# Running maxima of the scores in PSUM, later accumulating transfers, and a new chunk order in a fused attention block

## The chip, the core and the metric

The kernel runs on one core of a Trainium2 chip. The time is the device time of one execution in microseconds; the lower the better. A core has a matrix engine (TensorE, PE in the profile, with PEld for its weight loads), VectorE (DVE), ScalarE (ACT), GpSimd (POOL) and SyncE (SP), which issues transfers. Each runs its own queue in order; they wait for each other with semaphores. SBUF is the memory that they all work in, PSUM the small memory into which TensorE writes its products and which DVE and ACT can read and write too.

## The reference

One decoder block, batch 1, 1024 tokens with 16 learned meta tokens ahead of them (1040 rows), width 1024, all in float32.

```python
h = rmsnorm(concat([meta, x]), norm_g)
u_pool, z_pool, q, k, v, z_attn, f_logit, g_pool, g_attn = split(h @ w_in)
y_pool = causal_multiscale_pool(u_pool, pool_w, pool_scale) * silu(z_pool)
log_f  = log_sigmoid(f_logit + b_forget)
# logit[t, s] = q_t . k_s / 8 + sum of log_f over s < j <= t, causal; 8 heads of 64
y_attn = forgetting_attention(q, k, v, log_f) * silu(z_attn)
merged = sigmoid(g_pool) * (y_pool @ w_up_pool) + sigmoid(g_attn) * (y_attn @ w_up_attn)
out = rmsnorm(concat([meta, x]) + merged @ w_out, final_norm_g)[16:]
```

## The kernel before

**Arithmetic.** A float32 matrix is split into two parts of a reduced format, a rounded one and the rest (hh and hl of the normed rows, whi and wlo of a weight), and a product is three matmuls: hh x whi, hl x whi, hh x wlo. ACT makes whi (L156), POOL makes wlo with four subtractions of 256 columns (L158).

**Attention.** There are 16 units: four pairs of heads, two heads each, and two halves of 512 queries. A unit of the first half (even number) has five blocks of 128 keys, one of the second half (odd number) nine. `qk` makes the scores of one block: two matmuls (L680, L681) into one of two PSUM buffers ps, an addition of bias and mask on DVE for the diagonal part (L687), and an evacuation with bias on ACT (L689) into S in SBUF. The running maximum m over the blocks is an SBUF tile: at the second block DVE takes the maximum of the first two S (L693 copies columns that the second block doesn't reach, L694), and later m and S (L696). `maxes` finds the maximum over keys: DVE transposes m in squares of 32 (L701), reduces (L703), ACT swaps halves and quarters (L705, L708) with maxima on DVE between them (L706, L709), and DVE writes the result, spread over partitions, into a PSUM tile of the pool psT (L711). That pool has two buffers, called pt. `soft` subtracts it from S (L720), takes the exponential on ACT (L721), splits the result in ph (ACT, L724) and pl (DVE, L725, which reads S and ph, both in SBUF), adds up the denominators on POOL (acc, L730 to L733), and `av` multiplies ph and pl with V (L741) into po. `finish` copies po to SBUF (L748), stores both halves of it apart (y and y2, L750; their sum is wanted), and sums acc (L752, L754).

**Order.** PE's queue is written by hand: while unit i does `soft`, unit i+1 does `qk`, block by block, and a filler F puts matmuls of the input projection between the steps, also behind each unit's maxima, with the evacuations and splits that they need. The order on DVE, ACT, POOL and SP comes from a scheduler, bounded by `after` (stay behind an instruction in the same queue) and `behind` (wait for an instruction of another engine).

**Sums of blocks.** The gates' and the output's products are done as a 2 x 2 block scheme with seven products instead of eight, which needs sums of blocks of weights and of activations. They are made in device memory: SP stores blocks (put), ACT and POOL make negated blocks (neg, L602 and L604), and accumulating transfers on POOL's queue (`add`, L590, and `add_y`, L618, which sums y and y2 of a pair) add one to another. A table SUMS says which belong to which unit; `sums_of(i)` runs after `finish` of unit i, and the transfers stay behind the last acc addition in POOL's queue.

**Last block product.** Behind the attention come the block products (`g_prod`, L967) in four chunks of 512 rows each, whose PSUM tiles ga_[0..2] are pj buffers (three of them) and ga_[3] a pt buffer. The values that were in these buffers, the gate z of the pooling branch, are added to zp (`plus_`, L982, DVE) before the buffers are written again. `pool_mm(i)` multiplies the pooled values with their map and scales them (L848) into zp[i]; the last of the seven products, number 6, alternates with `pool_mm`, a chunk after a map. `up_weights` loads and splits a block of the next stage's weights (whu on ACT, L1098; wlu on DVE, L1099).

Of the kernel before, what the change touches and what calls it, by code (L numbers as in the profile page):

```python
# [8 lines left out]
F32 = mybir.dt.float32  # L9
F32R = mybir.dt.float32r  # L10
AF = mybir.ActivationFunctionType
ALU = mybir.AluOpType
# [42 lines left out]
def tile_hybrid_block(ctx, tc, x, meta, norm_g, w_in, b_forget, pool_w, pool_scale,  # L55
# [123 lines left out]
    def run(g):  # L179
        for _ in g:  # L180
            pass
# [406 lines left out]
    def add(dst, src):  # L588
        d, r = [t.rearrange("(p k) c -> p (k c)", k=4) for t in (dst, src)]
        after(nc.gpsimd.dma_start(d, r, accum_op=ALU.add, max_dma_last_dim=8192), accs[-1])  # L590
# [25 lines left out]
    def add_y(p):  # L616
        d, r = [spill[n, p].rearrange("(p k) c -> p (k c)", k=2) for n in ("y", "y2")]
        after(nc.gpsimd.dma_start(d, r, accum_op=ALU.add, max_dma_last_dim=8192), accs[-1])  # L618
# [26 lines left out]
    class Unit:  # L645
# [19 lines left out]
        def qk(self, b):  # L665
# [5 lines left out]
            if b == 0:  # L671
                self.m = ap_.tile([KB, 512], F32, name="m")
# [18 lines left out]
            if b == 1:  # L691
                if c0:
                    nc.vector.tensor_copy(m[:, :c0], S0[:, :c0])  # L693
                nc.vector.tensor_tensor(m[:, c0:], S0[:, c0:], s[:, c0:], op=ALU.max)  # L694
            elif b > 1:
                nc.vector.tensor_tensor(m[:kb, c0:], m[:kb, c0:], s[:kb, c0:], op=ALU.max)  # L696

        def maxes(self, extra=0.0):
            F.pull(LM1 + extra)
            mt = ap_.tile([KB, 512], F32, name="mt")  # L700
            nc.vector.transpose(mt, self.m)  # L701
            r, x, r2, y, mx = [sm.tile([128, 16], F32, name=n) for n in ("mr", "mx", "ms", "my", "mz")]
# [41 lines left out]
        def finish(self):  # L744
# [3 lines left out]
            nc.scalar.activation(t, po, AF.Copy)  # L748
            for n, part in (("y", hr), ("y2", lr)):
                nc.sync.dma_start(spill[n, self.p][hr, self.q0:self.q0 + 512], t[part])  # L750
# [35 lines left out]
    run(v_blocks(0, (6, 9), (0, 1)))  # L786
    units = [Unit(p, e, half) for p in range(4) for e in range(2) for half in range(2)]
    merged(list(units[0].a_steps()), [])
    units[0].maxes(FIRST)
    for i, u in enumerate(units):  # L790
# [11 lines left out]
        if nxt is not None:  # L802
            nxt.maxes()
        u.finish()
        sums_of(i)
        if i % 4 == 1 and i > 1:
            add_y(i // 4 - 1)
# [188 lines left out]
    add_y(3)  # L996
# [130 lines left out]
    ws[0, 0] = up_weights(0, 0)  # L1127
    plus_(zp[0][:, T1_], ga_[0])
    silu(zp[0][:, T1_], zp[0][:, T1_], -1.0)
    for i in range(4):  # L1130
        pool_mm(3 - i)
        g_prod(ga_[i], 6, i, False)
        if i:
            silu(za[i - 1][:, T1_], ga_[i - 1])
        if i < 2:
            rows_[i, 0] = gate_row(i, 0)
    silu(za[3][:, T1_], ga_[3])
# [209 lines left out]
```

## Time and profile before

| what | value |
|---|---|
| median of 3 runs | 745.23 us (744.98 to 746.96) |
| the profiled execution's own time | 744.3 us |
| its span in the profile | 742.6 us, mean granted clock of TensorE 0.996 |
| PE, PEld busy | 720.2 us (97%), 616.6 us (83%) |
| DVE, ACT, POOL busy | 536.5 us (72%), 417.0 us (56%), 334.4 us (45%) |

The page gives busy times of each engine; the idle time of an engine that isn't the bottleneck costs nothing. A row of a timeline reads: start in us, length in us, engine, line, operation, output <- inputs, shape, and x with the number of instructions that the row holds; in brackets the idle time of the engine before it, and the tile and engine that ended it. A row of groups has the count, then busy time in us, the mean of one in ns, and the idle time before them. Names in the profile leave out numbers: m, S, pt, pl and zp are the tiles above, pj a PSUM buffer of the projections.

### The profile page before, as it was taken

How to read it: one execution, taken by the hardware profiler on the slowest of the kernel's cores; microseconds unless marked ns; L12 is line 12 of the kernel's file. 1: busy time of each engine (PE TensorE's matmuls, PEld its weight loads, DVE VectorE, ACT ScalarE, POOL GpSimd, SP SyncE). 2: the span in 40 equal slices, each digit the busy share in tenths (PEclk: the TensorE clock that was granted, in tenths of full speed). 3: DMA queues.
4: the chain of work that ended last, by engine and by line, in shares of the span. 5: the costliest groups of instructions: out<-in, count | busy, mean ns of one | idle time of the engine just before them, and what ended most of it. 6: DMA issues, size and time to landing. Idle time of an engine off the chain costs nothing.

```text
span 742.6 us, 10841 instructions
## 1 busy us (share of the span) xinstructions
PE 720.2 (97%) x3637; PEld 616.6 (83%) x3637; DVE 536.5 (72%) x917; ACT 417.0 (56%) x914; POOL 334.4 (45%) x410
## 2 busy tenths in 40 slices
PE   8999999999999899999999999999989999999996
PEld 6997989997888797898988878888868888888885
DVE  4743577777889687887877858875876554887775
ACT  6752567565675666576765566342764432626445
POOL 4412245658336584365543766473843001005243
PEclk9999999999999999999999999999999999999999
DMA  9301125897864975738475586495905457672006
GB/s 285 77 26 32 29 67 194 206 330 170 221 194 92 237 202 161 192 68 208 124 173 120 134 214 229 117 342 174 307 16 170 143 184 258 222 266 76 0 1 227
DMA packets 88906, 120.45 MB, mean 162 GB/s; under 512 B 11377, under 2 KB 54385, under 8 KB 86786
## 3 DMA queue, kind: packets, MB, share of 16 engines
q1 hardware_dynamic: 85216, 100.36, 43.0%
q0 software_dynamic: 2336, 16.78, 12.2%
q10 hardware_dynamic: 1298, 2.63, 0.9%
q8 instruction: 28, 0.46, 0.3%
q14 instruction: 28, 0.23, 0.1%
HBM read 93.33 MB, written 54.72 MB: 199 GB/s over the span
## 4 chain that ended last, share of the span: by engine, by line
PE 71%; DVE 9%; ACT 8%; issue 4%; DMA 1%; POOL 0%; POOLq 0%; DVEq 0%; ACTq 0%; SPq 0%
PE pj L170 45%; PE pj L1227 8%; PE pj L967 6%; PE po L741 4%; PE pt L1227 2%; DVE pl L725 2%; PE pt L967 2%; PE ps L680 2%; ACT S L689 2%; PE ps L681 2%; ACT S L721 1%; ACT ph L724 1%; PE pj L515 1%; DVE m L696 1%; ACT whi L156 1%
## 5 line engine op out<-in xcount | busy, mean ns | idle before, releaser
L170 PE MATMUL pj<-hh,whi 128*128 128x512 f32 (+3 forms) x640 | 145.6, 354 | 0.0
L170 PE MATMUL pj<-hh,wlo 128*128 128x512 f32 (+3 forms) x640 | 143.6, 351 | 0.0
L170 PE MATMUL pj<-hl,whi 128*128 128x512 f32 (+3 forms) x640 | 142.7, 352 | 0.0
L158 POOL TENSOR_TENSOR wlo<-raw,whi 128x256 fp32r<-128x256 f32 x116 | 91.7, 871 | 97.9 <-ACT whi L156 41.5
L170 PEld LDWEIGHTS pj<-hl,whi 128*128 128x128 f32 x640 | 108.9, 190 | 12.0
L170 PEld LDWEIGHTS pj<-hh,whi 128*128 128x128 f32 x640 | 108.8, 190 | 11.8
L170 PEld LDWEIGHTS pj<-hh,wlo 128*128 128x128 f32 x640 | 108.6, 190 | 11.5
L725 DVE TENSOR_TENSOR pl<-S,ph 128x512 fp32r<-128x512 f32 (+4 forms) x112 | 89.3, 811 | 21.2 <-ACT ph L724 20.8
L733 POOL TENSOR_TENSOR acc<-acc,S 128x272 f32<-128x272 f32 (+4 forms) x80 | 76.7, 959 | 12.5 <-ACT S L721 6.6
L689 ACT ACTIVATE S<-ps,negc 128x400 f32<-128x400 f32 (+2 forms) x96 | 48.7, 515 | 47.9 <-DVE S L687 44.4
L696 DVE TENSOR_TENSOR m<-m,S 128x272 f32<-128x272 f32 (+4 forms) x80 | 47.6, 595 | 21.1 <-ACT S L689 18.9
L721 ACT ACTIVATE S<-S 128x512 f32<-128x512 f32 (+4 forms) x112 | 49.3, 478 | 17.2 <-DVE S L720 17.0
L724 ACT ACTIVATE ph<-S 128x512 fp32r<-128x512 f32 (+4 forms) x112 | 52.3, 479 | 7.2 <-PE po L741 6.9
L136 POOL TENSOR_TENSOR gw<-graw,gw 128x256 fp32r<-128x256 f32 x40 | 44.3, 1187 | 23.5 <-ACT gw L947 14.6
L720 DVE TENSOR_TENSOR S<-S,pt 128x512 f32<-128x512 f32 (+4 forms) x112 | 50.7, 498 | 0.6
L967 PE MATMUL pj<-gh,gw 128*128 128x512 f32 x180 | 43.7, 400 | 2.6 <-DVE zp L982 2.6
L680 PE MATMUL ps<-qa,ka 128*128 128x512 f32 (+4 forms) x112 | 37.6, 335 | 7.7 <-ACT S L689 7.5
L1120 DVE TENSOR_TENSOR rl<-pj,rl 128x512 f32<-128x512 f32 x32 | 22.0, 690 | 30.3 <-PE pj L170 30.2
L967 PEld LDWEIGHTS pj<-gh,gw 128*128 128x128 f32 x180 | 34.9, 194 | 10.5 <-issue 3.0
L156 ACT ACTIVATE whi<-raw 128x512 fp32r<-128x512 f32 x58 | 33.9, 622 | 12.6 <-PE pj L170 6.2
L741 PE MATMUL po<-pl,V 128*128 128x512 f32 (+4 forms) x112 | 38.1, 340 | 2.9 <-DVE pl L725 2.6
L731 POOL TENSOR_TENSOR acc<-S 128x400 f32<-128x400 f32 (+1 forms) x16 | 20.0, 1250 | 41.5 <-ACT S L721 41.4
(228 smaller groups left out, 1345.1 us busy)
## 6 DMA issues: line engine op xcount, KB each, us to landing
raw<-in_w_in_dram SPq DMA_DIRECT2D x31, 512.0 KB, 5.9
gs<-in_w_in_dram SPq DMA_DIRECT2D x5, 1024.0 KB, 6.9
td<-in_w_out_dram SPq DMA_DIRECT2D x5, 1024.0 KB, 10.6
xt<-in_x_dram SPq DMA_DIRECT2D x8, 512.0 KB, 7.8
sp_y<-t SPq DMA_DIRECT2D x32, 128.0 KB, 2.6
gs<-gs POOLq DMA_DIRECT2D x4, 1024.0 KB, 8.7
sp_gp<-st SPq DMA_DIRECT2D x16, 256.0 KB, 4.7
td<-td POOLq DMA_DIRECT2D x4, 1024.0 KB, 8.4
```

Of the source, the lines that this page charges most:

```text
L158: ins = nc.gpsimd.tensor_tensor(lo[:, k:k + 2], raw[:, k:k + 2], r32(hi[:, k:k + 2]), op=ALU.subtract)
L170: nc.tensor.matmul(ps, a, b, start=(i == 0), stop=(i == len(seq) - 1))
L680: nc.tensor.matmul(ps[:kb, c0:], ka[:, k0:k0 + kb], qa[:, q0 + c0:q0 + 512], start=True, stop=False)
L689: nc.scalar.activation(s[:kb, f0:], ps[:kb, f0:], AF.Identity, bias=nb_)
L696: nc.vector.tensor_tensor(m[:kb, c0:], m[:kb, c0:], s[:kb, c0:], op=ALU.max)
L721: exps.append(nc.scalar.activation(s[:kb, c0:], s[:kb, c0:], AF.Exp))
L724: nc.scalar.activation(ph[:kb, c0:], s[:kb, c0:], AF.Copy)
L725: dves.append(nc.vector.tensor_tensor(pl[:kb, c0:], s[:kb, c0:], r32(ph[:kb, c0:]), op=ALU.subtract))
L733: accs.append(nc.gpsimd.tensor_tensor(acc[:kb, c0:], acc[:kb, c0:], s[:kb, c0:], op=ALU.add))
L741: nc.tensor.matmul(self.po[:, c0:], v, r[:kb, c0:], start=(b == 0 and i == 0), stop=(b == self.nb - 1 and i == 1))
L967: nc.tensor.matmul(ps, op_w[n][p][k // 2][:, k % 2, i * 128:(i + 1) * 128], op_h[n][q][k // 2][:, k % 2], start=start and m == 0, stop=m = ...
L1227: nc.tensor.matmul(ps, pick(A_, k, p)[:, i * 128:(i + 1) * 128], pick(B_, k, q)[:, c0:c1], start=start and n == 0, stop=n == 11, skip_grou ...
```

## The change

It has four parts, and does the same arithmetic but for the place of one addition.

1. The running maximum m is a pt buffer in PSUM. ACT copies the first block's S into it; every later block is one maximum on DVE of m and S. The small tiles of the reduction (r, r2) are columns of the same buffer.
2. The accumulating transfers of unit i wait for the transpose of the next unit's maxima (a semaphore between DVE and POOL) instead of staying behind the last acc addition, and `sums_of(i)` and `add_y` are called from within `maxes` of unit i+1, ahead of `finish` of unit i.
3. For the last pair of heads, ACT copies one half of po, DVE adds the other, and one half is stored; the stores of y2 and `add_y(3)` are gone.
4. The last block product takes its chunks in the order 3, 2, 1, 0, and the weights `up_weights(0, 0)` come behind the last `plus_` and its silu.

PE's queue has the same 1880 rows in the same order, but for the PSUM buffers of the last product. In the changed kernel lines behind the first edit are moved by two to ten (the evacuation is L691, neg L604 and L606, `plus_` L992, the scaling L858, the weight split L1108, `g_prod` L977).

VectorE's queue ahead of the last product's maps, before (zp is the pooling gate, pt and pj its PSUM buffers, wlu the weight split):

```order
L982 TENSOR_TENSOR zp_5549<-pt_5537,zp_5549 128x512
L982 TENSOR_TENSOR zp_5547<-pj_5536,zp_5547 128x512
L982 TENSOR_TENSOR zp_5545<-pj_5535,zp_5545 128x512
L1099 TENSOR_TENSOR wlu_6124<-rawu_6121,whu_6123 128x512
L982 TENSOR_TENSOR zp_5543<-pj_5534,zp_5543 128x512
L848 SCALAR_TENSOR_TENSOR zp_5549<-pj_6131,psc_117,zp_5549 128x512
L848 SCALAR_TENSOR_TENSOR zp_5549<-pj_6139,psc_117,zp_5549 128x512
```

and now:

```order
L992 TENSOR_TENSOR zp_5525<-pt_5513,zp_5525 128x512
L992 TENSOR_TENSOR zp_5523<-pj_5512,zp_5523 128x512
L992 TENSOR_TENSOR zp_5521<-pj_5511,zp_5521 128x512
L992 TENSOR_TENSOR zp_5519<-pj_5510,zp_5519 128x512
L1108 TENSOR_TENSOR wlu_6101<-rawu_6098,whu_6100 128x512
L858 SCALAR_TENSOR_TENSOR zp_5525<-pj_6106,psc_117,zp_5525 128x512
L858 SCALAR_TENSOR_TENSOR zp_5525<-pj_6114,psc_117,zp_5525 128x512
```

The weight split has moved behind the fourth addition; the first product's chunk is now pt_5513 in PE's queue, the buffer of the first addition, where it was pj_5534, that of the fourth.

ScalarE's queue at the start of unit 3 (S is evacuated from ps; whi is a projection weight, st and neg are evacuations and a negated block), before:

```order
L689 ACTIVATE S_1788<-ps_1789,negc_116 128x512
L156 ACTIVATE whi_2041<-raw_2039 128x512 x2
L689 ACTIVATE S_1788<-ps_1817,negc_116 128x512
L352 ACTIVATE st_1834<-pj_1766 128x272
L689 ACTIVATE S_1828<-ps_1829,negc_116 128x512
L602 ACTIVATE neg_2070<-hh0_119 128x512
L689 ACTIVATE S_1828<-ps_1855,negc_116 128x512
```

and now:

```order
L691 ACTIVATE S_1783<-ps_1784,negc_116 128x512
L694 ACTIVATE pt_1782<-S_1783 128x512
L604 ACTIVATE neg_2002<-hh0_119 128x512
L156 ACTIVATE whi_2044<-raw_2042 128x512 x2
L691 ACTIVATE S_1783<-ps_1813,negc_116 128x512
L352 ACTIVATE st_1830<-pj_1770 128x272
L691 ACTIVATE S_1824<-ps_1825,negc_116 128x512
```

The copy into the maximum and neg have come ahead of whi and of the second evacuation.

GpSimd's queue behind unit 7's denominators (td3 and td5 are blocks of the output weights in device memory, wlo and neg parts of splits, acc the denominators of units 7 and 8), before:

```order
L733 TENSOR_TENSOR acc_3149<-acc_3149,S_3035 128x16
L590 DMA td3_778<-td5_780 128x2048
L158 TENSOR_TENSOR wlo_3391<-raw_3388,whi_3390 128x256 x4
L604 TENSOR_TENSOR neg_3446<-neg_3446,hl1_122 128x256 x2
L158 TENSOR_TENSOR wlo_3552<-raw_3549,whi_3551 128x256 x4
L730 COPY acc_3463<-S_3175 128x112
```

and now:

```order
L736 TENSOR_TENSOR acc_3137<-acc_3137,S_3025 128x16
L158 TENSOR_TENSOR wlo_3379<-raw_3376,whi_3378 128x256 x4
L606 TENSOR_TENSOR neg_3394<-neg_3394,hl1_122 128x256 x2
L590 DMA td3_778<-td5_780 128x2048
L158 TENSOR_TENSOR wlo_3539<-raw_3536,whi_3538 128x256 x4
L733 COPY acc_3450<-S_3163 128x112
```

The accumulating transfer has moved behind four splits and neg, and waits for the transpose of unit 8's maxima.

The diff:

```diff
--- before.py
+++ after.py
@@ -587,7 +587,9 @@
 
     def add(dst, src):
         d, r = [t.rearrange("(p k) c -> p (k c)", k=4) for t in (dst, src)]
-        after(nc.gpsimd.dma_start(d, r, accum_op=ALU.add, max_dma_last_dim=8192), accs[-1])
+        behind(nc.gpsimd.dma_start(d, r, accum_op=ALU.add, max_dma_last_dim=8192), trs[-1])
+
+    trs = []
 
     def put_h(n):
         put(rows_of(HS[n]), hblock(hh4, n))
@@ -615,7 +617,7 @@
 
     def add_y(p):
         d, r = [spill[n, p].rearrange("(p k) c -> p (k c)", k=2) for n in ("y", "y2")]
-        after(nc.gpsimd.dma_start(d, r, accum_op=ALU.add, max_dma_last_dim=8192), accs[-1])
+        behind(nc.gpsimd.dma_start(d, r, accum_op=ALU.add, max_dma_last_dim=8192), trs[-1])
 
     SUMS = {
         0: [(n21, 0), (put_h, "11")],
@@ -669,7 +671,7 @@
             d1 = max(0, min(512, b * KB + KB - t0))
             own_keys = b == NB - 1
             if b == 0:
-                self.m = ap_.tile([KB, 512], F32, name="m")
+                self.m = psT.tile([KB, 512], F32, name="pt")
             m = self.m
             if b % 2 == 0:
                 self.st = ap_.tile([KB, 2, 512], F32, name="S", tag="s", bufs=6)
@@ -688,18 +690,19 @@
             if f0 < 512:
                 nc.scalar.activation(s[:kb, f0:], ps[:kb, f0:], AF.Identity, bias=nb_)
             S0 = self.S[0]
-            if b == 1:
-                if c0:
-                    nc.vector.tensor_copy(m[:, :c0], S0[:, :c0])
-                nc.vector.tensor_tensor(m[:, c0:], S0[:, c0:], s[:, c0:], op=ALU.max)
-            elif b > 1:
+            if b == 0:
+                nc.scalar.activation(m, S0, AF.Copy)
+            else:
                 nc.vector.tensor_tensor(m[:kb, c0:], m[:kb, c0:], s[:kb, c0:], op=ALU.max)
 
-        def maxes(self, extra=0.0):
+        def maxes(self, extra=0.0, hook=None):
             F.pull(LM1 + extra)
             mt = ap_.tile([KB, 512], F32, name="mt")
-            nc.vector.transpose(mt, self.m)
-            r, x, r2, y, mx = [sm.tile([128, 16], F32, name=n) for n in ("mr", "mx", "ms", "my", "mz")]
+            tr = nc.vector.transpose(mt, self.m)
+            if hook is not None:
+                hook(tr)
+            r, r2 = self.m[:, :16], self.m[:, 16:32]
+            x, y, mx = [sm.tile([128, 16], F32, name=n) for n in ("mx", "my", "mz")]
             nc.vector.tensor_reduce(r, mt.rearrange("p (j b) -> p j b", b=32), axis=AX.X, op=ALU.max)
             for a, b in ((0, 64), (64, 0)):
                 nc.scalar.activation(x[a:a + 64], r[b:b + 64], AF.Copy)
@@ -745,8 +748,12 @@
             hr, lr = rows(self.e)
             po, acc = self.po, self.acc
             t = ap_.tile([128, 512], F32, name="t")
-            nc.scalar.activation(t, po, AF.Copy)
-            for n, part in (("y", hr), ("y2", lr)):
+            if self.p == 3:
+                nc.scalar.activation(t[hr], po[lr], AF.Copy)
+                nc.vector.tensor_tensor(t[hr], po[hr], t[hr], op=ALU.add)
+            else:
+                nc.scalar.activation(t, po, AF.Copy)
+            for n, part in (("y", hr), ("y2", lr))[:1 if self.p == 3 else 2]:
                 nc.sync.dma_start(spill[n, self.p][hr, self.q0:self.q0 + 512], t[part])
             at = ap_.tile([KB, 512], F32, name="mt")
             after(nc.vector.transpose(at, acc), dves[-1])
@@ -784,6 +791,12 @@
     pair_fill(1)
     gates()
     run(v_blocks(0, (6, 9), (0, 1)))
+    def sums_at(i, tr):
+        trs.append(tr)
+        sums_of(i)
+        if i % 4 == 1 and i > 1:
+            add_y(i // 4 - 1)
+
     units = [Unit(p, e, half) for p in range(4) for e in range(2) for half in range(2)]
     merged(list(units[0].a_steps()), [])
     units[0].maxes(FIRST)
@@ -800,11 +813,8 @@
             after(nc.scalar.activation(pwh, pw, AF.Copy), exps[-1])
             nc.gpsimd.tensor_tensor(pwl, pw, r32(pwh), op=ALU.subtract)
         if nxt is not None:
-            nxt.maxes()
+            nxt.maxes(hook=lambda tr: sums_at(i, tr))
         u.finish()
-        sums_of(i)
-        if i % 4 == 1 and i > 1:
-            add_y(i // 4 - 1)
         if i == 13:
             g_raw0 = [gp.tile([128, 2, 512], F32, name="graw", tag="g") for _ in range(2)]
             for k in range(2):
@@ -993,7 +1003,6 @@
         U[g] = gp.tile([128, L], F32, name="u", tag="g")
         nc.sync.dma_start(U[g], spill["u", g])
 
-    add_y(3)
     w_in_(1)
     u_in(3)
     h_in(2)
@@ -1124,17 +1133,17 @@
             gt[j] = sg_
 
     ws, rows_ = {}, {}
-    ws[0, 0] = up_weights(0, 0)
     plus_(zp[0][:, T1_], ga_[0])
     silu(zp[0][:, T1_], zp[0][:, T1_], -1.0)
-    for i in range(4):
-        pool_mm(3 - i)
+    ws[0, 0] = up_weights(0, 0)
+    for n, i in enumerate((3, 2, 1, 0)):
+        pool_mm(i)
         g_prod(ga_[i], 6, i, False)
-        if i:
-            silu(za[i - 1][:, T1_], ga_[i - 1])
-        if i < 2:
-            rows_[i, 0] = gate_row(i, 0)
-    silu(za[3][:, T1_], ga_[3])
+        if n:
+            silu(za[i + 1][:, T1_], ga_[i + 1])
+        if n < 2:
+            rows_[n, 0] = gate_row(n, 0)
+    silu(za[0][:, T1_], ga_[0])
     ws[1, 0] = up_weights(1, 0)
     M2.close()
 
```

## The prediction

> **What bounds the kernel now.** I read the page's first part, then what PE waits for, then the stretch around the longest wait.
>
> ```profile
> PE 720.2 (97%) x3637; PEld 616.6 (83%) x3637; DVE 536.5 (72%) x917; ACT 417.0 (56%) x914; POOL 334.4 (45%) x410
> ```
>
> PE is busy in 97% of the span of 742.6 us, and its matmuls stay what they are. So the change can only take away PE's waits, or slow clock, or add waits. The waits of PE by tile (tile, line, releaser: total us, how many, longest) are these in the attention:
>
> ```profile
> PE ps L680 <- ACT S L689: 7.5, 11, 1.9
> PE po L741 <- DVE pl L725: 2.6, 3, 1.5
> ```
>
> Together 10.1 us. One more stands in the last block product; both places are touched.
>
> **The last product.** The windows of PE (stretch, length, busy, granted clock) and the timeline there:
>
> ```profile
> 553.20:555.70 2.50, 0.00 (x0) 1.00 0.00 0
> 555.70:558.00 2.30, 2.28 (x6) 0.52 0.00 0
> 558.00:560.30 2.30, 2.30 (x9) 0.74 0.00 0
> ```
>
> ```profile
> 551.19 0.68 DVE L982 TENSOR_TENSOR zp<-pt,zp 128x512 f32<-128x512 f32 x1
> 551.79 1.28 DVE L982 TENSOR_TENSOR zp<-pj,zp 128x512 f32<-128x512 f32 x2
> 554.29 0.69 DVE L1099 TENSOR_TENSOR wlu<-rawu,whu 128x512 fp32r<-128x512 f32 x1 [1.22 <-ACT whu L1098]
> 554.89 0.68 DVE L982 TENSOR_TENSOR zp<-pj,zp 128x512 f32<-128x512 f32 x1
> 555.50 1.40 DVE L848 SCALAR_TENSOR_TENSOR zp<-pj,psc,zp 128x512 f32<-128x512 f32 x2
> 555.72 4.58 PE L967 MATMUL pj<-gh,gw 128*128 128x512 f32 x12 [2.60 <-DVE zp L982]
> 561.53 2.92 PE L967 MATMUL pj<-gh,gw 128*128 128x512 f32 x12
> ```
>
> The reader is to see one queue order. Before the change the first chunk of the last product overwrites the buffer that DVE frees last, at 554.89 + 0.68, and that addition stands behind the weight split L1099, which waits for ACT. PE stands still for 2.60 us, and the twelve matmuls behind it take 4.58 us at a granted clock of 0.52 to 0.74; the next chunk's twelve take 2.92. With the new order the first product goes into the pt chunk, which is freed at 551.19 + 0.68 = 551.87, before PE's work ahead of it ends (555.72 − 2.60 = 553.1). So wait and low clock both go: 2.60 + (4.58 − 2.92) = **4.26 us**. What is late next is the buffer of the third pool matmul: DVE still has to do the fourth addition, the split and two L848 (now L858). With the addition ahead of the split (no longer delayed by it) the split at 554.29 sets when they start: 554.29 + 0.69 + 1.40 = 556.4, against PE's 553.1 + 2.92 plus about 1.2 of a pool matmul's work. Enough, by less than a microsecond. Later chunks use their buffers in the same rhythm as now.
>
> The Trainium skill, "TensorE: Matmul & The Clock Gate", Part 1 (the HAM clock gate), says the clock falls after an idle window of about 3.4 us; by it a gap of 2.6 us need not cost clock, and the sum would hold 2.60 and not 4.26. The window rows show 0.52 right behind the gap, so I take the measurement, and keep that outcome as a rival.
>
> **Stalls of VectorE in the attention.** Three of PE's longer waits each go back to one DVE instruction stretched to several times its length:
>
> ```profile
> 179.64 4.17 DVE L696 TENSOR_TENSOR m<-m,S 128x272 f32<-128x272 f32 x1 [0.45 <-ACT S L689]
> 184.21 0.39 PE L741 MATMUL po<-pl,V 128*128 128x272 f32 x1 [1.45 <-DVE pl L725]
> 196.64 0.81 POOL L590 DMA_DIRECT2D hsX<-hs  x1
> 197.62 3.22 DVE L694 TENSOR_TENSOR m<-S 128x512 f32<-128x512 f32 x1 [1.20 <-ACT S L689]
> 206.69 0.33 PE L680 MATMUL ps<-qa,ka 128*128 128x144 f32 x1 [1.34 <-ACT S L689]
> 274.83 0.81 POOL L590 DMA_DIRECT2D td<-td  x1
> 275.36 5.04 DVE L725 TENSOR_TENSOR pl<-S,ph 128x512 fp32r<-128x512 f32 x1 [0.16 <-ACT ph L724]
> 275.39 3.07 POOL L158 TENSOR_TENSOR wlo<-raw,whi 128x256 fp32r<-128x256 f32 x4
> 280.45 0.50 PE L741 MATMUL po<-pl,V 128*128 128x512 f32 x1 [0.87 <-DVE pl L725]
> ```
>
> Each stretched instruction reads two SBUF operands just after POOL issued an accumulating DMA. The change acts twice on this. The maximum now reads one PSUM and one SBUF operand, like L720, whose mean stays short with the same neighbours:
>
> ```profile
> L720 DVE TENSOR_TENSOR S<-S,pt 128x512 f32<-128x512 f32 x48 | 31.2, 681 | 0.6
> L696 DVE TENSOR_TENSOR m<-m,S 128x512 f32<-128x512 f32 x24 | 19.7, 821 | 10.6 <-ACT S L689 9.2
> ```
>
> And the DMAs move behind the next unit's transpose of the maxima, where DVE's next work reads one operand or PSUM. One DMA stands there already, and the transpose after it isn't stretched:
>
> ```profile
> 235.25 1.05 POOL L618 DMA_DIRECT2D sp_y<-sp_y  x1
> 236.21 0.71 DVE L701 STREAM_TRANSPOSE mt<-m 128x512 f32<-128x512 f32 x1
> ```
>
> So I drop the three waits: 1.45 + 1.34 + 0.87 = **3.66 us**. The operation PSUM,SBUF into PSUM is not in the trace; its bounds are 0.681 (L720, which writes SBUF) and 0.821 (L696 as it is); I take 0.68, since L720 has the same operands. Either way the 24 x 0.14 us less are DVE time, off PE's path except where counted. The small steps behind the transpose (reduce, half swaps, two maxima) now touch PSUM; their cost I bound by ±0.1 us a step, an estimate from 0.14, hidden by the filler matmuls that the program puts behind each unit's maxima.
>
> **What ACT pays.** Each of the 16 units gets one copy S to PSUM on ACT. It is not in the trace; between 0.598 (below, PSUM to SBUF) and 0.63 (L602 below, SBUF to SBUF); I take 0.60, for the nearer end.
>
> ```profile
> L748 ACT ACTIVATE t<-po 128x512 f32<-128x512 f32 x16 | 9.6, 598 | 4.2 <-PE po L741 4.0
> 196.92 0.67 ACT L689 ACTIVATE S<-ps,negc 128x512 f32<-128x512 f32 x1
> 198.23 0.39 PE L680 MATMUL ps<-qa,ka 128*128 128x512 f32 x1
> 150.17 0.50 PE L680 MATMUL ps<-qa,ka 128*128 128x512 f32 x1 [0.36 <-ACT S L689]
> 244.43 0.48 SPq L586 DMA_DIRECT2D hsC<-neg  x1
> 248.16 0.63 ACT L602 ACTIVATE neg<-hh 128x512 f32<-128x512 f32 x1 [1.93 <-POOL wlo L158]
> 249.42 0.50 PE L680 MATMUL ps<-qa,ka 128*128 128x512 f32 x1 [1.95 <-ACT S L689]
> 345.75 0.50 PE L680 MATMUL ps<-qa,ka 128*128 128x512 f32 x1 [0.41 <-ACT S L689]
> ```
>
> Where the copy stands between the first two evacuations of a unit, it fits if PE comes later: in unit 5 the second evacuation ends at 196.92 + 0.67 = 197.59 and PE needs it at 198.23, 0.64 us of slack, so the copy is free; units 9 and 13 have the same order, and I take the same for them; units 1 and 15, where neighbours move too, I leave at nothing. At the starts of units with five blocks PE has no wait in the list, since steps of the nine-block unit before lie between their blocks. Where PE waits already (unit 3 at 150.17, unit 11 at 345.75) there is no slack. In unit 3 copy and the moved neg both come ahead of the second evacuation: 0.60 + 0.63 = **+1.23**. In unit 11 the copy alone: **+0.60**. In unit 7 neg (248.16) waited 1.93 us for its buffer's store, issued at 244.43, with the evacuation behind it; store and neg are now issued earlier, neg ahead of the first evacuation: −1.95 + 0.63 = **−1.32**.
>
> **Moved, at nothing.** An add now waits for a transpose of DVE, and behind it on POOL stand weight splits and the next sums acc. The longest time that an add moves back is from 438.69 to 449.98, 11.3 us; a split has more lead than that (420.22 + 3.38 = 423.6 to its use at 437.05, 13.5 us), and most splits now stand ahead of the add. If a split came later than its matmul, PE would pay the difference.
>
> ```profile
> 420.22 3.38 POOL L158 TENSOR_TENSOR wlo<-raw,whi 128x256 fp32r<-128x256 f32 x4
> 437.05 0.61 PE L170 MATMUL pj<-hh,wlo 128*128 128x512 f32 x2
> 438.69 0.84 POOL L590 DMA_DIRECT2D td<-td  x1
> 449.98 0.71 DVE L701 STREAM_TRANSPOSE mt<-m 128x512 f32<-128x512 f32 x1
> ```
>
> In pair 3, four additions on DVE (at most 0.68 each, as L720, together 2.7 us), four stores and one DMA go or come, at places where PE's list of waits names nothing; I cost them at zero.
>
> **Sum.** −4.26 − 3.66 + 1.23 + 0.60 − 1.32 = −7.41. The profiled run took 744.3, so 736.9; the median of the runs before (745.23) is 0.93 above the profiled one, so **737.8 us**.
>
> **Rivals.** One place of the timeline belongs to the first: four splits on POOL with no DMA issued near them, and a maximum beside them.
>
> ```profile
> 149.35 3.71 POOL L158 TENSOR_TENSOR wlo<-raw,whi 128x256 fp32r<-128x256 f32 x4
> 150.15 1.17 DVE L694 TENSOR_TENSOR m<-S 128x512 f32<-128x512 f32 x1 [1.41 <-ACT S L689]
> ```
>
> - *The stalls follow the splits, not the DMA.* The row of POOL at 275.39 speaks for it: its four splits run while pl is held, and they stay near. Then the maxima, no longer with two SBUF operands, are cured, and pl is not: 0.87 stays, 738.7. The Trainium skill, "SBUF — State Buffer", Who interferes with whom, has this rule: a VectorE instruction with two SBUF inputs contends with a GpSimd instruction that reads SBUF, and the later one blocks fully. Against it: splits with no DMA issue near them hold nothing for long. The maximum above, beside four splits, took 1.17 us and not 3.22.
> - *The DMAs' shadow moves with them* and falls on other two-operand instructions (pl of the next unit, ql and ka of the projections), or POOL comes late: nothing of 3.66 is won, 741.5. For: the place behind the transpose is only a few steps long. Against: the rows at 235.25.
> - *All waits of the attention close* (10.1 us), since the chain to the evacuations gets shorter: 744.3 − 4.26 − 10.1 + 0.93 = 730.9. Against: rows such as 249.42 come from ACT's order, not from stalls.
> - *The last product gets a new wait* (the pool matmul's buffer above, less than a microsecond of margin, or the moved weight split) that eats the gain: 742.1.
> - *The low clock comes from elsewhere*, and only 2.60 goes: 739.5.
> - *Slower:* ACT's copy delays the second evacuation in every unit, because slack such as 0.64 is used up by evacuations now in step with PE: 16 x 0.60 = 9.6 on PE's path, no stall won: 745.23 − 4.26 + 9.6 = 750.6. It decides from 4.26 / 0.60, eight copies, on. For: units 3 and 11. Against: unit 5's slack, and units with five blocks.
>
> **How the numbers follow.** Forecast 0.45; splits 0.10; shadow moved 0.20; all closed 0.08; new wait 0.06; clock 0.04; slower 0.07. A measurement tells 0.3%, 2.24 us, so below 743.0 is faster. Forecast, splits, all closed and clock lie below, and most of the shadow and new-wait cases; a part of these (0.05), of the forecast (0.03) and of the slower case (0.02) falls within: 0.84, 0.10, 0.06. The range goes up over the moved shadow and the new wait with the 0.7 us that remain to the bound, 742.8, and down to 733.0: the two unit costs (1.83) not landing and 3 of the other 5.1 us of waits closing. Left out: the slower case, all closed, and a rest.
>
> **What would show it.** In the changed profile: no wait of PE ahead of the last product and its clock near 1; maxima of 128x512 near 0.68 us, none above 1; POOL's DMA issues right behind transposes and no pl of several microseconds after them; waits of PE at the starts of units 3 and 11 longer by 1.2 and 0.6, at unit 7 shorter. A new wait of PE for wlo, for a neg or for zp would make it wrong, as would waits for S at the start of most units.

## The result, and the profile after

| | before | changed |
|---|---|---|
| median | 745.11 us (744.41 to 746.96, 4 runs) | 734.57 us (734.52 to 735.55, 4 runs) |
| ratio, 95% interval | | 0.9858 [0.9838, 0.9877] |
| profiled execution, span | 744.3 us, 742.6 us | 734.6 us, 732.9 us |

The change takes 10.5 us (1.4%) off. The forecast was 737.8 us, 7.4 us off. From the page of the changed kernel and its list of PE's waits (tile, line, releaser: us in total, how many, longest):

```profile
PE 714.6 (98%) x3637; PEld 615.7 (84%) x3637; DVE 506.5 (69%) x913; ACT 422.1 (58%) x930; POOL 326.9 (45%) x409
```

```profile
PE ps L682 <- ACT S L691: 9.1, 8, 5.5
PE pn L414 <- DVE car L550: 1.3, 1, 1.3
```

The reader is to see three things: the waits for pl and for zp are gone from the list; those for S, which were 7.5 us with a longest of 1.9, are now 9.1 with one of 5.5; and PE's busy time fell by 5.6 us (720.2 to 714.6) although its matmuls are the same. By the two traces 1.8 us of that lie in the last product and 1.5 at the start, both told below, and most of the rest where waits went; behind the new wait at unit 3 it rose by 1.4.

Both kernels run the same 3,637 matmuls in the same order. So the start of each matmul after, less its start before, shows stretch by stretch where time went (worked out from the two traces, times of the profile before):

| stretch of the profile before | change of the difference, us | what stands there |
|---|---|---|
| 0 to 20 | −1.78 | the start, untouched by the change |
| 98 to 106 | −1.80 | unit 1's first evacuations |
| 146 to 156 | +6.37 | unit 3's first evacuations |
| 156 to 236 | −3.05 | −1.72 at 184, −0.80 at 207, −0.54 at 232 |
| 245 to 250 | −2.93 | unit 7's first evacuations |
| 278 to 289 | −1.98 | −1.17 at 280, the rest up to 289 |
| 294 to 300 | +1.58 | unit 9's first evacuations |
| 300 to 550 | −1.91 | several places, none above 1.2 |
| 550 to 560 | −4.44 | the last product |
| sum | −9.94 | |

**The start** is not the change's. The windows from 11.50 to 16.50 (stretch, length, busy and number of matmuls, clock, share of the DMA engines, GB/s) of before, and then of after:

```profile
11.50:16.50 5.00, 5.00 (x24) 1.00 1.11 335
```

```profile
11.50:16.50 5.00, 4.76 (x38) 1.00 1.10 332
```

In the same 5 us the profiled run of before did 24 matmuls, the other 38. The clock column says 1.00 for both, since the trace records the granted clock only from 16.48 us on before, and from 11.53 on after. In the profiles of the twelve kernels below that record starts at 10.3 to 12.9 us, and they are 0.5 to 1.8 us ahead of the one profile of before, among them kernels that leave everything near the start as it was. So that one run most likely came to full clock late.

**The last product**, in the changed kernel's timeline:

```profile
545.49 0.68 DVE L992 TENSOR_TENSOR zp<-pt,zp 128x512 f32<-128x512 f32 x1
546.09 1.88 DVE L992 TENSOR_TENSOR zp<-pj,zp 128x512 f32<-128x512 f32 x3
547.46 2.90 PE L977 MATMUL pt<-gh,gw 128*128 128x512 f32 x12
550.19 0.40 PE L170 MATMUL pj<-plh,pwh 128*128 128x512 f32 x1
```

No bracket stands behind the product: PE goes on without a wait, its twelve matmuls take 2.90 us instead of 4.58, and the pool matmul behind them doesn't wait either.

**Unit 3**, where the changed kernel loses, by its timeline, the list of transfers in that stretch (KB, us to landing) and two windows of PE:

```profile
141.49 0.49 SPq L586 DMA_DIRECT2D hsA<-neg  x1
149.05 0.63 ACT L604 ACTIVATE neg<-hh 128x512 f32<-128x512 f32 x1 [4.52 <-DMA hsA<-neg]
150.63 0.67 ACT L691 ACTIVATE S<-ps,negc 128x512 f32<-128x512 f32 x1
151.34 0.79 PE L682 MATMUL ps<-qa,ka 128*128 128x512 f32 x1 [5.47 <-ACT S L691]
```

```profile
hsA<-neg SPq DMA_DIRECT2D x1, 256.0 KB, 7.5
```

```profile
148.00:151.30 3.30, 0.00 (x0) 0.51 1.05 303
151.30:154.90 3.60, 3.56 (x10) 0.50 1.05 322
```

The tile neg has one buffer. The store of the block before it is issued at 141.49 and lands 7.5 us later. Until then ScalarE waits with neg at the head of its queue, the evacuation behind it is late, PE stands still for 5.47 us, and its next matmuls run at half clock. The slow store goes with part 2: in the nine kernels of this case whose weight and activation transfers keep their place, or are left out, it lands here in 2.5 to 2.6 us, and in the five with late transfers, this one among them, in 5.5 to 8.1 (5.5 in adds_late, which differs from the kernel before by nothing else). Full DMA engines alone don't explain it: in the profile before their share was 0.97 while it landed. Unit 9 has the same on a smaller scale:

```profile
291.09 0.63 ACT L604 ACTIVATE neg<-hh 128x512 f32<-128x512 f32 x1 [2.16 <-DMA hsC<-neg]
292.35 0.50 PE L682 MATMUL ps<-qa,ka 128*128 128x512 f32 x1 [0.71 <-ACT S L691]
```

**The maxima**, in the groups of VectorE and ScalarE of the attention:

```profile
L696 DVE TENSOR_TENSOR pt<-pt,S 128x512 f32<-128x512 f32 x32 | 22.4, 700 | 37.7 <-ACT S L691 37.2
```

```profile
L694 ACT ACTIVATE pt<-S 128x512 f32<-128x512 f32 x16 | 9.6, 599 | 0.3
```

A maximum takes 700 ns where it took 821 and 1684, and the copy takes 599, as forecast (0.68 and 0.60).

### The profile page after: what moved, and what is told of

Same layout as the page of the kernel before. It is cut to its first block, busy times and chain, and to the rows that moved or that the text cites. A ratio compares the mean times of both kernels' runs of the same rounds, so it can differ in the third digit from the quotient of the medians.

```text
span 732.9 us, 10808 instructions
## 1 busy us (share of the span) xinstructions
PE 714.6 (98%) x3637; PEld 615.7 (84%) x3637; DVE 506.5 (69%) x913; ACT 422.1 (58%) x930; POOL 326.9 (45%) x409
## 4 chain that ended last, share of the span: by engine, by line
PE 83%; DMA 3%; ACT 3%; DVE 2%; issue 1%; POOL 1%; SPq 0%; POOLq 0%; ACTq 0%; DVEq 0%
PE pj L170 51%; PE pj L1236 8%; PE pj L977 8%; PE po L744 5%; PE pt L977 3%; PE pt L1236 2%; PE ps L683 2%; PE ps L682 2%; PE pj L515 1%; DMA hsA<-neg 1%; DMA hsC<-neg 1%; DMA graw<-in_w_in_dram 1%; POOL acc L736 1%; ACT S L691 1%; DMA raw<-in_w_in_dram 1%
## 5 line engine op out<-in xcount | busy, mean ns | idle before, releaser
L158 POOL TENSOR_TENSOR wlo<-raw,whi 128x256 fp32r<-128x256 f32 x116 | 88.8, 815 | 75.4 <-PE pj L170 25.2
L728 DVE TENSOR_TENSOR pl<-S,ph 128x512 fp32r<-128x512 f32 (+4 forms) x112 | 83.9, 759 | 26.2 <-ACT ph L727 25.5
L696 DVE TENSOR_TENSOR pt<-pt,S 128x400 f32<-128x400 f32 (+2 forms) x96 | 46.7, 487 | 50.3 <-ACT S L691 48.7
L736 POOL TENSOR_TENSOR acc<-acc,S 128x272 f32<-128x272 f32 (+4 forms) x80 | 74.7, 933 | 14.3 <-ACT S L724 9.0
L691 ACT ACTIVATE S<-ps,negc 128x400 f32<-128x400 f32 (+2 forms) x96 | 48.6, 514 | 39.1 <-DVE S L689 34.9
L977 PE MATMUL pj<-gh,gw 128*128 128x512 f32 x180 | 42.0, 390 | 0.0
L977 PEld LDWEIGHTS pj<-gh,gw 128*128 128x128 f32 x180 | 33.8, 188 | 7.1
L683 PE MATMUL ps<-ql,ka 128*128 128x512 f32 (+4 forms) x112 | 37.8, 338 | 0.0
```

What stands on the lines that cost most here:

```text
L158: ins = nc.gpsimd.tensor_tensor(lo[:, k:k + 2], raw[:, k:k + 2], r32(hi[:, k:k + 2]), op=ALU.subtract)
L683: nc.tensor.matmul(ps[:kb, c0:], ka[:, k0:k0 + kb], ql[:, q0 + c0:q0 + 512], start=False, stop=True)
L691: nc.scalar.activation(s[:kb, f0:], ps[:kb, f0:], AF.Identity, bias=nb_)
L728: dves.append(nc.vector.tensor_tensor(pl[:kb, c0:], s[:kb, c0:], r32(ph[:kb, c0:]), op=ALU.subtract))
L736: accs.append(nc.gpsimd.tensor_tensor(acc[:kb, c0:], acc[:kb, c0:], s[:kb, c0:], op=ALU.add))
L977: nc.tensor.matmul(ps, op_w[n][p][k // 2][:, k % 2, i * 128:(i + 1) * 128], op_h[n][q][k // 2][:, k % 2], start=start and m == 0, stop=m = ...
```

## The experiments

All times are medians; the kernel before ran beside each group with medians of 743.55 to 744.57 us. In single runs it went from 740.25 to 749.63, so places are read from the matmul starts, not from medians alone.

### The two losses: neg_third

```diff
-        after(nc.scalar.activation(t, hblock(hh4, blk)[:, k], AF.Copy, scale=-1.0), exps[-1])
+        after(nc.scalar.activation(t, hblock(hh4, blk)[:, k], AF.Copy, scale=-1.0), thirds[-1])
...
-                nc.scalar.activation(s[:kb, f0:], ps[:kb, f0:], AF.Identity, bias=nb_)
+                ev = nc.scalar.activation(s[:kb, f0:], ps[:kb, f0:], AF.Identity, bias=nb_)
+                if b == 2:
+                    thirds.append(ev)
```

(`ev` is the evacuation; the dots stand for the lines between, and the line that makes the list `thirds` is not shown.)

> The changed kernel, with each negation on ScalarE bound behind the evacuation of the third block of the next unit. Theory (the changed trace: at unit 3 the moved negation waits 4.52 us for the store of its single buffer, with the evacuations queued behind it, and PE waits 5.47 us; at unit 9 it waits 2.16 us): both PE waits go, with the slow clock behind the first, 6.1 + 1.5 us less against the changed kernel's 734.6, so 726 to 729. Rival (ScalarE is late there because of the new copy into PSUM, and the negation only stands in the same gap): 732 to 735, with a wait of several us left at unit 3. Rival (the wait moves behind the third evacuation and hits the fourth): 730 to 734, PE waiting at the fifth block.

Measured: **726.25 us** (726.06 to 727.65), ratio to before 0.9753 [0.9729, 0.9776]. The starts of the matmuls leave those of the changed kernel at two places by more than 0.2 us, −6.6 us at unit 3 and −1.6 at unit 9. The waits of PE:

```profile
PE ps L682 <- ACT S L691: 2.5, 5, 1.3
PE pn L414 <- DVE car L550: 1.3, 1, 1.3
```

So the place of neg in ScalarE's queue, and not the copy, made both losses. This version beats both kernels, and its interval doesn't touch the changed kernel's.

### Part 4 and its halves: only_last, only_chunks, only_upw

The edits are those of the diff in the last block: the whole part, the chunk order alone, the place of `up_weights(0, 0)` alone, each on the kernel before.

> The kernel before with part 4 alone (chunk order 3, 2, 1, 0 and the weights behind the last addition). Theory: the 2.6 us wait and the half clock behind it go together, 4.3 to 4.5 us, so 740.6 to 740.9. Rival (the low clock comes from elsewhere and stays): 742.5. Rival (the pool matmul's buffer takes the wait's place): 743 to 745.

> The kernel before with the chunk order 3, 2, 1, 0 alone; the weights' split stays ahead of the fourth addition. Theory: the first product writes the early pt buffer, so the 2.6 us wait and the slow clock go; the fourth addition ends at about 555.6 and the two scalings about 557, so the third pool matmul waits about 0.4 us: 3.9 to 4.3 us gained at this place. Rival (what mattered was the split ahead of the addition): the wait stays above 1.5 us.

> The kernel before with the weights' split moved behind the fourth addition alone; the chunk order stays 0, 1, 2, 3. Theory: the fourth addition follows the third, 553.1 + 0.7 = 553.8 in the clock of the profile before, so PE's wait falls from 2.6 to about 0.6 us plus the semaphore, and the clock does not fall: 3.4 to 3.8 us gained at this place. Rival (the clock falls after any wait here): 2.0 gained, windows of 0.5 granted clock behind it.

Measured: 739.05 us, ratio 0.9924 [0.9896, 0.9951], for the whole part; 739.98 and 740.35 in one run each for the halves. At the place itself the starts gain 4.4 us by the whole and by the chunk order alone, a little more than was expected of the latter, and 3.7 by the weights alone. The first product in the two halves, chunk order first:

```profile
553.11 2.90 PE L967 MATMUL pt<-gh,gw 128*128 128x512 f32 x12
```

```profile
553.35 3.00 PE L967 MATMUL pj<-gh,gw 128*128 128x512 f32 x12 [0.50 <-ACT zp L979]
```

Either edit takes away the wait and the slow clock with it; the first does it wholly, and the wait of 0.4 us that I expected of it at the third pool matmul didn't come. The two are not additive.

The slow clock doesn't belong to the wait as such, though. Six of the profiles have the old order and a wait of 2.4 to 2.6 us here. In four of them half clock follows; in no_adds and only_hook, below, it doesn't. Their first product, no_adds first, and PE's window of no_adds:

```profile
548.29 2.96 PE L967 MATMUL pj<-gh,gw 128*128 128x512 f32 x12 [2.40 <-DVE zp L982]
```

```profile
563.65 3.00 PE L974 MATMUL pj<-gh,gw 128*128 128x512 f32 x12 [2.41 <-DVE zp L989]
```

```profile
548.20:551.20 3.00, 2.91 (x13) 1.00 0.00 0
```

So 2.6 us of part 4's gain are the wait, and 1.7 a slow clock that some runs have here and others don't; the last section tells on what that depends.

### Part 1 alone: only_psum

> The kernel before with part 1 alone (maximum in PSUM, copy by ScalarE). Theory: the stretched maxima go, PE's waits at 184, 206 and 329 with them (1.45 + 0.85 + 0.3 at least), the held pl at 275 stays, and copies cost 0.6 us each at units 3 and 11: 742 to 744. Rival (the sixteen copies land on PE's path): 748 to 754. Rival (the stretched instructions are not released by the PSUM operand): 745 to 747, a maximum of over 3 us in the trace.

Measured: 739.25 us, ratio 0.9923 [0.9897, 0.995], more than expected; yet not for the reason given. The wait at 184 stays. Timeline of this kernel there, and its waits for pl:

```profile
175.23 0.80 POOL L590 DMA_DIRECT2D hs<-hsl  x1 [0.21 <-issue]
175.61 4.91 DVE L724 TENSOR_TENSOR pl<-S,ph 128x272 fp32r<-128x272 f32 x1
180.58 0.39 PE L740 MATMUL po<-pl,V 128*128 128x272 f32 x1 [1.40 <-DVE pl L724]
```

```profile
PE po L740 <- DVE pl L724: 5.1, 5, 2.1
```

The maximum, now with one PSUM operand, is not held; the next instruction with two SBUF operands is, just behind the same transfer. The wait at 206 does go (−0.8 us by the starts). The gain came at units 1 and 7 (−1.7 and −2.9), where ScalarE's queue had changed with the maximum, and at unit 15 (−1.7); a pl held for 4.18 us at 225 gives 3.7 us of it back.

### What holds VectorE: no_adds

The body of `add` is left out (`pass`), so the sums of blocks are not made; `add_y` and all splits stay.

> The kernel before with the thirteen accumulating transfers of weight and activation blocks left out (the sums of blocks are not made; add_y stays). All splits on GpSimd stay. Theory (the transfers): the holds at 179, 197, 275 and 391 go, the longest single maximum or pl of VectorE is under 2.5 us, PE's waits for pl fall from 2.6 to under 0.5 us. Rival (the splits): at least two of these instructions still take over 3 us beside a run of splits.

Measured: 735.68 us in one run. The holds at 179, 197, 275 and 391 are gone, with every split where it was. In the attention one instruction takes over 3 us by itself, behind one of the four transfers that are left:

```profile
411.69 0.77 POOL L618 DMA_DIRECT2D sp_y<-sp_y  x1 [0.32 <-PE pj L170]
412.03 3.70 DVE L725 TENSOR_TENSOR pl<-S,ph 128x400 fp32r<-128x400 f32 x1
```

So splits alone don't make the holds; the accumulating transfer is needed. It doesn't hold alone either. In the profile before, GpSimd's next instruction behind the transfer at 345.13 starts at 347.09, and the maximum between them takes its plain 0.69 us:

```profile
345.13 0.82 POOL L590 DMA_DIRECT2D hsC<-hsB  x1 [0.25 <-PE ps L681]
345.73 0.69 DVE L694 TENSOR_TENSOR m<-S 128x512 f32<-128x512 f32 x1 [1.50 <-ACT S L689]
```

In all fourteen profiles an instruction with two SBUF operands that starts within 2 us of a transfer with nothing right behind it takes 0.69 us at most. Where GpSimd goes on right behind the transfer, the held instruction ends about when that work does: with two instructions of GpSimd there it takes up to 2.1 us, with four up to 3.7, with six up to 5.3, and with eight 6.9 (an addition of 128x1037 in the pooling branch, behind the last `add_y`, where its plain time is 1.2). So the transfer opens the hold, and the work queued behind it sets its length.

### Calls early, transfers early or late: only_hook, adds_late

Two halves of part 2 on the kernel before: the calls moved into `maxes` with the transfers still behind the last acc; and the transfers behind the transpose with the calls where they were (the last pair's `add_y` keeps its place).

> The kernel before with only the place of the calls changed: sums_of and add_y called from within the next unit's maxima, the transfers still behind the last acc addition. Theory: the negations come ahead of the first evacuations, the one of unit 3 waits for its buffer's store and costs PE about 6 us, that of unit 9 about 1.5, while unit 7 gains about 1.9: 749 to 752. Rival (the negation waits only because the later accumulating transfers or the copies shift the stores): 743 to 746, no wait of PE above 2 us at unit 3.

> The kernel before with the accumulating transfers bound behind the transpose of the next unit's maxima, and nothing else moved: the calls stay behind finish, so the negations stay where they were; the maximum is in SBUF. Theory (the transfer's issue is what holds two-operand instructions of VectorE): the holds at 179, 197 and 275 go, no VectorE instruction of 128x272 or more takes over 3 us by itself in the units, PE's waits for pl (2.6 us) and the one at 206 go: 740 to 742.5 against 744.6. Rival (the splits on GpSimd hold them): the holds stay where splits run, 744 to 746.

Measured: 748.64 us, ratio 1.0049 [1.0029, 1.0069], and 752.05 us, ratio 1.0113 [1.0066, 1.016]. Both halves of part 2 are slower by themselves. only_hook loses 3.5 us at unit 3 and not 6: its neg waits 0.29 us there, since the store lands in 2.6 us. The long wait needs the late transfers, which slow the store, as well. Unit 9 loses nothing in it, and unit 7, where a gain of 1.9 was expected, loses 1.5: its neg waits 1.82 us for the store there, and half clock follows. For adds_late the expectation missed by 10 us. The wide holds are gone, as it said (no wide VectorE instruction of the units over 2 us by itself); but two other things came, first neg again, at unit 7:

```profile
247.72 0.63 ACT L604 ACTIVATE neg<-hh 128x512 f32<-128x512 f32 x1 [4.73 <-DMA hsC<-neg]
248.98 0.79 PE L682 MATMUL ps<-qa,ka 128*128 128x512 f32 x1 [4.42 <-ACT S L691]
```

and second, holds on a tiny instruction, which the next experiments single out.

### What the place of the maxima does: sbuf_max, small_psum

sbuf_max is neg_third with part 1 undone. small_psum is sbuf_max with this edit:

```diff
-            r, x, r2, y, mx = [sm.tile([128, 16], F32, name=n) for n in ("mr", "mx", "ms", "my", "mz")]
+            mw = psT.tile([128, 512], F32, name="pt")
+            r, r2 = mw[:, :16], mw[:, 16:32]
+            x, y, mx = [sm.tile([128, 16], F32, name=n) for n in ("mx", "my", "mz")]
```

> The kernel of neg_third with part 1 undone: the maximum in SBUF again, the transfers behind the transposes, the negations behind the third evacuation. Theory (with the transfers moved, a maximum of two SBUF operands is no longer held, so part 1 only saves what the plain durations save and pays the copies): within 3 us of neg_third's 726.3, 725 to 729.5, no maximum over 2 us in the trace. Rival (the PSUM operand is what cures the holds): 731 or more, holds of over 3 us on maxima.

Measured: 739.08 us, ratio 0.9935 [0.9916, 0.9955]; the theory missed by 10 us. No wide maximum is held. But behind the transposes, where the transfers now stand, comes the small maximum ms <- mr, mx of 128 x 16, with two SBUF operands. Its timeline at unit 11, and PE's wait that follows:

```profile
326.75 0.81 POOL L590 DMA_DIRECT2D gs<-gs  x1 [6.68 <-DVE mt L705]
328.56 2.67 DVE L712 TENSOR_TENSOR ms<-mr,mx 128x16 f32<-128x16 f32 x1
338.17 0.50 PE L682 MATMUL ps<-qa,ka 128*128 128x512 f32 x1 [2.24 <-ACT S L691]
```

Four splits stand right behind that transfer; at the units where none does, the same step takes 0.18 us at most. It is on the way to everything that `soft` does, so ScalarE's whole queue is late by it.

> The kernel of sbuf_max (running maximum in SBUF, transfers behind the transposes, negations behind the third evacuation) with one edit: the two small tiles of the reduction (128 x 16) are columns of a pt buffer in PSUM, as in the changed kernel. Theory (what is held at the transfers' new place are the small maxima of two SBUF tiles, 2.67 us at 328.56 and 2.71 us at 447.31 in sbuf_max, with PE's wait of 2.24 us and a half clock behind the first): both holds go, 4.1 and 3.5 us less than sbuf_max's 739.1, so 730.5 to 733. Rival (the wide maxima's SBUF operand and place make all of the distance to neg_third): 737 to 740. Rival (the small tiles make all of it): 726 to 728.

Measured: 732.25 us (730.8 to 733.13), ratio 0.9847 [0.9813, 0.9881], inside what was expected. The small maximum at that place:

```profile
328.61 0.16 DVE L714 TENSOR_TENSOR pt<-pt,mx 128x16 f32<-128x16 f32 x1
```

From 2.67 us to 0.16; by the starts of the matmuls 4.0 us are gained there and 3.6 at unit 15. So part 1's small tiles in PSUM are what makes the transfers' new place free of holds. The other 6.0 us between small_psum and neg_third lie at the start (0.7, a matter of the run) and at units 1, 3, 6 and 15, by the starts of the matmuls, and these belong to the wide maximum and the copy; at unit 3 ScalarE waits 3.3 us for a store of u there. How that hangs together with the maximum stays open.

### Part 2 undone, and neg alone: adds_back, neg_only

adds_back is the changed kernel with calls and transfers of before; neg_only is the kernel before with the edit of neg_third.

> The changed kernel with part 2 undone: calls and transfers where they were before, the maximum in PSUM, the last product and the last pair as changed. Theory (the holds then fall on pl, as in only_psum; the negations no longer stand ahead of the evacuations): the wait of 5.5 us at unit 3 is gone, waits for pl of 5 us in all come back, 733 to 736, that is about what the changed kernel takes. Rival (part 2 as it was made is what brings the gain in the attention): 738 or more. Rival (part 2 only costs): 729 or less.

> The kernel before with only the negations bound behind the third evacuation of the unit whose scores are running. Theory: the waits of PE behind negations go, at unit 1 (1.13 us) and unit 7 (1.95 us) with the slow clock that sometimes follows, while all holds of VectorE stay: 740 to 742.5 against 743.8 to 744.6. Rival (these waits come from the evacuation's place in ScalarE's queue alone, whatever the negation does): 743 to 745.

Measured: 734.78 us, ratio 0.9882 [0.9846, 0.9918], and 739.24 us, ratio 0.9931 [0.9903, 0.9958]. In adds_back the hold of pl is back:

```profile
269.80 0.81 POOL L590 DMA_DIRECT2D td<-td  x1
270.06 5.32 DVE L728 TENSOR_TENSOR pl<-S,ph 128x512 fp32r<-128x512 f32 x1 [0.64 <-ACT ph L727]
275.44 0.50 PE L744 MATMUL po<-pl,V 128*128 128x512 f32 x1 [0.82 <-DVE pl L728]
```

and the wait at unit 3 is gone. At 734.78 it takes what the changed kernel takes (734.57): part 2 as it was made gives back at units 3 and 9 what it gains elsewhere. neg_only gains more than expected. The wait of 1.95 us at unit 7 is gone, so neg ahead of evacuations already cost the kernel before. But PE's waits for pl at 184 and 280 are gone too (−1.7 and −1.1 us by the starts), though no transfer has moved: neg's part on GpSimd now comes later. In the profile before it stands right behind the four splits that hold pl at 275:

```profile
278.19 1.66 POOL L604 TENSOR_TENSOR neg<-neg,hl 128x256 f32<-128x256 f32 x2
```

In neg_only it doesn't, and pl takes 3.67 us where it took 5.04:

```profile
271.69 0.81 POOL L590 DMA_DIRECT2D td<-td  x1
272.22 3.67 DVE L729 TENSOR_TENSOR pl<-S,ph 128x512 fp32r<-128x512 f32 x1 [0.16 <-PE po L745]
272.25 3.08 POOL L158 TENSOR_TENSOR wlo<-raw,whi 128x256 fp32r<-128x256 f32 x4
279.36 1.56 POOL L606 TENSOR_TENSOR neg<-neg,hl 128x256 f32<-128x256 f32 x2 [4.03 <-ACT neg L604]
```

At 184 the hold falls on a later pl, for which PE doesn't wait.

## Why the prediction was right, and where it was not

The time lies in the range, the direction is right, and the size is short by 3.1 us. By its terms:

- **Last product: −4.26, measured −4.44.** Right, by the mechanism named, for the wait. The other 1.66 of the term, the slow clock, I took from one profile; two of six kernels with that wait have none (no_adds, only_hook), so that it was there to be won in this pair of profiles is partly luck.
- **Three stalls: −1.45, −1.34, −0.87; measured −1.72, −0.80, −1.17.** The sum, 3.66 against 3.69, is right. The cause is right in that the transfer is needed (no_adds) and that moving it cures the wide holds (adds_late); what the prediction lacks is that GpSimd's work right behind the transfer is needed too and sets the length (neg_only). The part given to the wide maximum was wrong: with a PSUM operand alone the hold goes to pl (only_psum). I named the small steps behind the transpose and gave them ±0.1 us; with SBUF tiles one of them was held for 2.67 us (sbuf_max). The edit that I priced at nothing protects the place.
- **Unit 3: +1.23, measured +6.37.** This is the step that failed. "In unit 3 copy and the moved neg both come ahead of the second evacuation: 0.60 + 0.63" counts what neg takes and leaves out what it waits for. The trace before had it: neg started at 151.49 after a wait of 0.51 us for the store of its buffer, so with the store where it stood it could not start at 148.4, where the order put it. That alone prices the step near 3 us. The store's 7.5 us to landing, which goes with the late transfers (2.6 without them), and the half clock made the rest.
- **Unit 9: nothing, measured +1.58.** The same omission.
- **Unit 7: −1.32, measured −2.93.** Right in kind. (The row at 248.16 names a split of GpSimd and not the store, which the prediction read as the cause; it is the store, since in every kernel where neg waits here it starts 0.1 to 0.4 us behind the store's landing, also in adds_late, whose row names the store.) The neg that I charged with 0.63 us starts there without a wait, and PE doesn't wait behind it:

```profile
243.46 0.62 ACT L604 ACTIVATE neg<-hh 128x512 f32<-128x512 f32 x1
244.28 0.39 PE L682 MATMUL ps<-qa,ka 128*128 128x512 f32 x1
```

- **Unit 11: +0.60, measured −0.1. Unit 1: nothing, measured −1.80.** The copy was hidden there; in only_psum and adds_back, where the transfers keep their place, it costs 0.63 us at unit 11, as priced. At unit 1 neg moved from ahead of the second evacuation to behind the third, which the order would have shown had I priced each start by what stands between the evacuations.
- **Parts at nothing.** From 450 to 550 us, where the last two of the four additions and the missing transfer stand, the starts keep one distance within 0.1 us, so these cost and gain nothing on PE's path. Part 3 was not tried alone.
- **Rivals.** The shadow of the transfers doesn't move to wide instructions, it would have moved to small ones. Splits as the only cause fall by no_adds, yet the rival was half right: they set how long a hold lasts. A slow clock that comes from elsewhere is half right too, as said of the last product. The sixteen copies don't land on PE's path, but for the one at unit 11 in two of the experiments.

The attention as a whole was forecast at −3.15 and came to −3.72 (−9.94 + 1.78 + 4.44): two errors of over 6 us in all at units 3 and 9 against gains at units 1 and 7 and small ones that I hadn't counted. The sum is better than its terms, and that is luck. Without the start the two profiles differ by 8.2 us and the medians by 10.5; the other 2.4 us lie in what varies between the runs of the kernel before, and the runs don't show where.

## What to carry to other kernels

An instruction that is moved ahead costs what it takes and what it waits for at the new place: look in the trace when its buffer came free, and who stands behind it in its queue. When a disturbance is moved, look at the smallest instructions at its new place too; a 128 x 16 step on a chain that all wait for can cost more than a wide one beside the path. Two traces with the same matmuls are best compared by the starts of the same matmul, which also tells a late start of one run from a gain.

## What the runs showed of the hardware

**The clock.** In all fourteen profiles the recorded changes of the granted clock lie on a grid of 3.41 us, whose place against the program's start differs from profile to profile. Every stretch of half clock in the middle of the program lasted one or two of its steps, 3.41 or 6.83 us. It came behind 11 of the 14 waits of PE of 2.1 to 5.5 us, and in 4 stretches behind the 43 waits of 0.9 to 2.0 us. Adding up PE's idle time in each step of the grid tells them apart: all 13 steps at full clock with over half of it idle (0.53 to 1.00) were followed by half clock, two of the seven with 0.43 to 0.49 were, and none with less. So the wait of 2.60 us ahead of the last product, of which one step held 0.76 of its length in the profile before, was followed by half clock, and the one of 2.40 in no_adds, spread over two steps with 0.35 each, was not. The shortest wait with such a stretch behind it was 1.12 us, in only_chunks, together with smaller ones in the same step:

```profile
97.90:101.10 3.20, 1.79 (x11) 1.00 0.00 0
101.40:104.80 3.40, 3.40 (x15) 0.50 0.15 58
104.80:108.00 3.20, 3.20 (x20) 1.00 0.15 44
```

The same wait of 1.1 us at this place had no such stretch in six other kernels. So a short wait costs itself and, by where it falls on the grid, some 1.7 us more (half of 3.41), an estimate from these stretches. That is one source of the scatter from run to run: the kernel before took 740.25 us in a run with a mean granted clock of 0.999, and 749.63 in one with 0.990. The Trainium skill, "TensorE: Matmul & The Clock Gate", Part 1 (the HAM clock gate), has free-running windows of 3413 ns, which the grid agrees with, and lets the clock fall after a whole idle window, which the waits of 1.12 to 2.75 us ahead of such stretches don't bear out.

**VectorE.** An instruction with two SBUF operands that started within about 2 us of the issue of an accumulating transfer on GpSimd, with other work of GpSimd right behind that issue, could be held until about the end of this work: for up to 5.3 us in the attention (adds_back), however small it was (128 x 16 took 2.67 us in place of 0.16). Not every one was: in the profile before, a pl of 128 x 400 that starts at 419.55, 0.4 us behind such an issue, and ends before GpSimd's next splits begin, took its plain 0.57 us. With nothing right behind the issue none was held (0.69 us at most), and with no transfer issued ahead of it none in the attention took over 1.81 us beside such work. With one operand in PSUM none was held.
